# The page table of the paged cache, read as whole rows in an earlier stage

## The chip, the core and the metric

The program runs on one core of a Trainium2 chip. A core has a matrix engine (PE in the profile, with its weight loads shown apart as PEld), three engines for element work (DVE, ACT and POOL), and SP, which here only issues transfers (the row "SPq" of a profile is its issuing of one). The metric is the device time of one execution in microseconds (us). The kernel before took 2102.95, 2104.4 and 2106.95 us in three runs, median 2104.4.

## What is computed

The reference is one inference step of a small trunk of two layers, in float32. Layer 0 is a Mamba-2 mixer, layer 1 is multi-head latent attention (MLA). A prompt of 1024 tokens and 8 sampled sequences of 8 new tokens each go through the same parameters; the sampled sequences have 2048 old tokens each, held in a cache of pages of 128 tokens:

```python
h = h + Mixer_i(RMSNorm(h))            # i = 0: Mamba-2, i = 1: MLA; then a final RMSNorm
cache_ckv  (1, N_POOL, 128, 256)       # paged key/value latents
cache_kpe  (1, N_POOL, 128, 32)        # paged rotary keys
page_table (8, 16) int32               # logical page -> physical page, one row per sequence
```

The page table is what matters for this change. The 128 entries, one for each page of each sequence, say which physical pages belong to the 8 sequences. The kernel turns them into addresses at two places. The rotary keys of all 128 pages are gathered with the 128 entries as they stand, one for each of the 128 partitions. The latents are gathered later in pieces of four pages (512 tokens): sequence b, piece q takes the entries b·16 + 4q + 0 to 3. For this the kernel wants a table of indices with 128 partitions and 32 columns. Column 4b + q belongs to one piece; partition 32j + s holds 32 · page_table[b, 4q + j] + s, so a page is fetched as 32 rows of four tokens. It needs, in partitions 32j to 32j + 31, every fourth entry of the flat page table, starting with the j-th.

## The kernel before

Layer 0 takes the first part of the program, layer 1 the rest. Layer 1 begins with the input stage, `mla_in`. It first normalises the rows of the residual and transposes them in three groups of token tiles (`norm_steps`, `norm_cols`). For each group and each of 8 slices of 128 columns, PE transposes three token tiles into a PSUM tile `xtp` (L234), ACT writes the high part `hh` from it (L235), and DVE writes the low part `hl`, which is the rest that the rounding of `hh` leaves (L236). The products in this stage are three-part sums of high and low parts, which is why each tensor comes as a pair. The `xtp` tiles have three PSUM buffers in turn, so the transposes for slice 3 wait until `hl` of slice 0 has been written, those for slice 4 wait for `hl` of slice 1, and so on. The gate products `pj` (L88) of the same stage are interleaved with the transposes of the next group.

Then `gather_kpe` loads the 128 page-table entries as one column (`kpidx`, L1351) and POOL issues the indirect gather of the rotary keys into `kprows` (L1353). PE transposes those rows a little later (`kpt`, L1362).

After further projections the stage comes to `mla_cq` and `mla_q`. `mla_cq` forms the normalised query latent tile by tile. The last transposed tile passes through a buffer `cqs` (L991) and is split into `cqh` (ACT, L129) and `cql` (DVE, L130). The very last, 64-row tile is folded: ACT copies one half of a PSUM tile into an SBUF tile `pq` (L111), DVE adds the other half (L112). That SBUF tile shares the single buffer of `cqs`, so the copy at L111 waits until `cql` has been computed from it. `mla_q` multiplies the query latent by its weights (PE, `pq`, L100); the result goes through `qt` (ACT, L1012), gets its rotation on DVE (L1018 to L1021), and is stored in DRAM as `q_d` by SP (L1022). `qt` has two buffers, so the third `qt` waits for the first store to land. Between these products the first head group is prepared: the weights `w` are loaded (L1109, L1111) and split (L129, L130), and PE forms the values `vp` (L88). The PSUM tile of `vp` comes from the same three buffers that the folded tile occupies.

The table of indices for the latents is built in `Sample.__init__`, which stands in the program after `mla_q`. It loads the page table with four transfers into 32 partitions each (`ptab`, L1379), each taking every fourth entry, then loads a column of slot numbers (`pslot`, L1381), converts the table to float (`ptf`, L1383), multiplies and adds (L1384) and converts back (`ptidx`, L1386). The first gather that uses it comes in the sampled part of the attention, over 400 us later.

The order of the instructions on DVE, ACT and SP is not written out by hand at this place. A scheduler orders them by its own estimate of when operands are ready, so an instruction may stand earlier in its engine's queue than its text in the program. Each engine then takes its own queue strictly in order, and a waiting instruction holds up all that stand behind it. That is how the loads of `ptab` come to be issued, and `ptf` to be computed, in the middle of `mla_cq` and `mla_q`.

Of the kernel before, what the change touches and what calls it, by code (L numbers as in the profile page):

```python
# [8 lines left out]
F32 = mybir.dt.float32  # L9
F32R = mybir.dt.float32r  # L10
AF = mybir.ActivationFunctionType
ALU = mybir.AluOpType
# [6 lines left out]
NB = 8  # L19
# [17 lines left out]
NPG = PAST // PAGE  # L37
# [649 lines left out]
def h_loader(k):  # L687
    def load(xt, i):
        t0, m = TILES[i]
        k.nc.sync.dma_start(xt[:m], k.h_d[t0 : t0 + m])  # L690

    return load
# [174 lines left out]
def mla_in(k, right, mid):  # L867
    tc, nc, I = k.tc, k.nc, k.I
    k.g_d = k.dram.tile([8, 128, T], F32, name="g_d")
    with ExitStack() as st:  # L870
        xp = st.enter_context(open_pool(tc, name="hT", bufs=1))
        k.xh = xp.tile([128, 8, T + 64], F32R, name="hh")
        k.xl = xp.tile([128, 8, T], F32R, name="hl")

        rw = st.enter_context(open_pool(tc, name="rw", bufs=1))
        sg = ExitStack()
        wg = sg.enter_context(open_pool(tc, name="wpg", bufs=1))
        with k.h0, open_pool(tc, name="h1", bufs=1, side="right") as p0:
            first = [gate_block(k, wg, rw, 0), gate_block(k, wg, rw, 1)]
            norm_steps(k, h_loader(k), k.normc[1], k.xh, k.xl, p0, k.psum, first, 3, tail=True)  # L880
            for b in first:
                next(b, None)
        mp = k.mps.enter_context(open_pool(tc, name="mp", bufs=1, side="right"))
        k.kvh = mp.tile([128, 2, SEQ], F32R, name="kvh")
        k.kvl = mp.tile([128, 2, SEQ], F32R, name="kvl")
        k.kvs = [k.cm.tile([128, 2, 64], F32R, name=f"kvs{x}") for x in "hl"]
        gates = (None for b in range(2, 8) for _ in gate_block(k, wg, rw, b))
        with open_pool(tc, name="kg", bufs=1, side="right") as kg:
            gk = gather_kpe(k, kg)
            next(gk)  # L890
            for n in range(QG + 8):
                next(gates)
                if n >= QG:
                    next(gk)
            drain(gk)
        kp = right.enter_context(open_pool(tc, name="kTp", bufs=1, side="right"))
        k.kT = (kp.tile([98, SEQ], F32R, name="kTh0"), kp.tile([98, SEQ], F32R, name="kTl0"))
        hp = mid.enter_context(open_pool(tc, name="hp", bufs=1, side="right"))
        k.cqh = hp.tile([128, 4, T + 64], F32R, name="cqh")
        k.cql = hp.tile([128, 4, SEQ], F32R, name="cql")  # L900
        sp = mid.enter_context(open_pool(tc, name="sp2", bufs=1, side="right"))
        wk = ExitStack()
        wkp = wk.enter_context(open_pool(tc, name="wpk", bufs=1, side="right"))
        wkv = load_cw(k, wkp, rw, 512, 288, "ck")
        drain(gates)
        sg.close()
        wq = st.enter_context(open_pool(tc, name="wpc", bufs=1))
        wcq = load_cw(k, wq, rw, 0, 512, "cw")
        mla_kv(k, sp, wkv)
        wk.close()  # L910
        wu = mid.enter_context(open_pool(tc, name="wu1", bufs=1, side="right"))
        k.wu = wu
        k.wu0 = load_w(k, wu, I["mla_w_uq"][0].rearrange("q h e -> q (h e)")[:, :384], 4, 384, "wq", 1, None, 1)
        mla_cq(k, sp, wcq)
# [380 lines left out]
def drain(g):  # L1295
    for _ in g:
        pass
# [71 lines left out]
        k.kpe_d.append(d)  # L1369


class Sample:
    def __init__(self, k, pool):
        nc, I = k.nc, k.I
        self.k, self.sp = k, None
        pt = pool.tile([128, 32], mybir.dt.int32, name="ptab")
        for j in range(4):
            src = I["page_table"].rearrange("b (q j) -> j (b q)", j=4)[j : j + 1].to_broadcast([32, 32])
            nc.sync.dma_start(pt[32 * j : 32 * j + 32], src)  # L1379
        ps = pool.tile([128, 1], F32, name="pslot")  # L1380
        nc.sync.dma_start(ps, I["c_slot"])  # L1381
        pf = pool.tile([128, 32], F32, name="ptf")
        nc.vector.tensor_copy(pf, pt)  # L1383
        nc.vector.tensor_scalar(pf, pf, 32.0, ps, op0=ALU.mult, op1=ALU.add)  # L1384
        self.idx = pool.tile([128, 32], mybir.dt.int32, name="ptidx")
        nc.vector.tensor_copy(self.idx, pf)  # L1386
        self.items = [(b, q) for b in range(NB) for q in range(4)]
        self.raw, self.hl, self.cT, self.tk = {}, {}, {}, {}
        self.state, self.held, self.new, self.ps = {}, {}, {}, {}
# [403 lines left out]
def layer_mla(k):  # L1793
    tc, nc = k.tc, k.nc
    k.og_d = k.dram.tile([8, 128, SEQ], F32, name="og_d")
    k.npool = k.I["cache_ckv"].shape[1]
    with ExitStack() as st:
        k.q_d = k.dram.tile([T, MH * 96], F32, name="q_d")
        PB.update(PB2)
        k.cm = st.enter_context(open_pool(tc, name="cm", bufs=1))  # L1800
        right, mid, heads, k.mps = ExitStack(), ExitStack(), ExitStack(), ExitStack()
        p2 = ExitStack()
        k.psum = p2.enter_context(open_pool(tc, name="ps2", bufs=1, space=PS))
        mla_in(k, right, mid)
        qp = st.enter_context(open_pool(tc, name="qp", bufs=1))
        k.qlh = qp.tile([128, 2, NB, 128], F32R, name="qlh")
        k.qll = qp.tile([128, 2, NB, 128], F32R, name="qll")
        k.qpr = qp.tile([96, NB, 128], F32R, name="qpr")
        k.mr = qp.tile([128, 256], F32R, name="mr")
        early = ExitStack()  # L1810
        hd = Heads(k, early)
        q0 = ExitStack()
        hd.start(q0)
        early_units = [hd.prep_kv(0)] * 13 + [hd.prep_q(0)] * 5 + [hd.maxpass(0, 0)] * 6
        early_units += [hd.prep_q(1)] * 5 + [hd.maxpass(0, 1)] * 10
        done = 0
        for n, _ in enumerate(mla_q(k, mid)):
            while done < min((n - Q0 + 1) * len(early_units) // (33 - Q0), len(early_units)):
                next(early_units[done], None)
                done += 1  # L1820
        q0.close()
        mid.close()
        p2.close()
        psum = heads.enter_context(open_pool(tc, name="ps3", bufs=1, space=PS))
        hd.open(heads, psum)
        sm = Sample(k, qp)
        with tc.manual_schedule(engines={nc.tensor.engine, nc.gpsimd.engine}):
            flow = mla_heads(k, hd, sm, early, st)
        heads.close()
        right.close()  # L1830
        with tc.manual_schedule(engines={nc.tensor.engine, nc.gpsimd.engine}):
            mla_sample(k, sm, flow)
        k.mps.close()
# [59 lines left out]
```

## Time and profile before

| | |
|---|---|
| runs (us) | 2102.95, 2104.4, 2106.95; median 2104.4 |
| span of the profiled execution | 2095.4 us; the page gives no other time for that execution, so the runs lie 7.6 to 11.6 above it (median 9.0) |
| mean granted clock of PE | 0.969 of full speed |
| DVE busy | 1340.1 us (64%) |
| ACT busy | 1043.3 us (50%) |
| POOL busy | 851.9 us (41%) |
| data moved | 207.61 MB, 99 GB/s on average |

A timeline row gives start and duration of an instruction or of a run of equal ones, the engine, line and operation, the tiles written and read, the shape, and in brackets how long the engine had been idle before it and what ended that idle time. A row of the chain of waits is one link of the chain of work that ended last: the link's start, its duration and its engine or transfer. A row of the waits by engine names the waiting instruction, then the one that released it, then the total idle time, the number of times and the longest. Durations of matmuls overlap, so their pace is read from the distance of their starts.

### The profile page before, as it was taken

To read this page: it belongs to the slowest core of one execution; us is meant where nothing else is said; L and a number is where in the kernel's file an instruction comes from. 1 tells how busy PE (TensorE), PEld (TensorE's weight loads), DVE (VectorE), ACT (ScalarE), POOL (GpSimd) and SP (SyncE) were. 2 spreads that over 40 slices of the span, in tenths; PEclk is the share of its full clock that TensorE was granted. 3 is DMA by queue.
4 is the path that set the end of the run, shared out by engine and by line. 5 is a ranking of instruction groups with operands and counts; after the bars stand their busy time and mean duration, and the time that the engine had idled before them with its cause. 6 is when DMAs were issued, how large, how long until landed. Compare 5 with 4: busy or idle time off the path is not lost.

```text
span 2095.4 us, 33766 instructions
## 1 busy us (share of the span) xinstructions
PE 1948.3 (93%) x12001; PEld 1763.6 (84%) x12001; DVE 1340.1 (64%) x2838; ACT 1043.3 (50%) x2287; POOL 851.9 (41%) x1059
## 2 busy tenths in 40 slices
PE   6999999999999999789998999699999999889998
PEld 5898999899999998677787998698888888778887
DVE  4558676767676767865334314366787778776665
ACT  5455565556565656522114323234676667755552
POOL 0337564646664646744000001102343334765541
PEclk9999999999999999889999999899999989999999
DMA  4222324231324241635534342132111112464451
GB/s 144 56 59 64 111 66 115 56 114 57 105 66 115 56 115 46 208 122 192 183 124 133 124 152 63 52 108 68 48 55 52 43 37 61 133 197 131 142 152 40
DMA packets 187631, 207.61 MB, mean 99 GB/s; under 512 B 23260, under 2 KB 153064, under 8 KB 187080
## 3 DMA queue, kind: packets, MB, share of 16 engines
q1 hardware_dynamic: 182408, 185.67, 29.2%
q0 software_dynamic: 4976, 19.66, 3.0%
q8 instruction: 95, 1.56, 0.3%
q14 instruction: 72, 0.59, 0.1%
q10 hardware_dynamic: 80, 0.13, 0.0%
HBM read 152.10 MB, written 53.28 MB: 98 GB/s over the span
## 4 chain that ended last, share of the span: by engine, by line
PE 33%; DVE 9%; issue 4%; POOL 4%; DMA 3%; ACT 2%; SPq 0%; POOLq 0%; DVEq 0%; ACTq 0%
PE pq L100 5%; PE pob L100 5%; PE pj L88 4%; PE poa L100 2%; POOL kvl L1541 2%; PE pk L100 1%; PE p L100 1%; PE vp L88 1%; PE st L1246 1%; DVE tl L1260 1%; PE st L1248 1%; PE st L1247 1%; PE o L1277 1%; PE sc L1214 1%; PE kp L88 1%
## 5 line engine op out<-in xcount | busy, mean ns | idle before, releaser
L88 PE MATMUL pj<-xh,wih 128*128 128x384 f32 (+1 forms) x768 | 254.9, 336 | 10.9 <-ACT xh L235 6.6
L88 PE MATMUL pj<-xl,wih 128*128 128x384 f32 (+1 forms) x768 | 255.9, 333 | 0.0
L88 PE MATMUL pj<-xh,wil 128*128 128x384 f32 (+1 forms) x768 | 255.1, 332 | 0.0
L1260 POOL TENSOR_TENSOR tl<-P,th 128x384 fp32r<-128x384 f32 (+1 forms) x96 | 90.7, 945 | 181.0 <-ACT P L1258 138.5
L88 PEld LDWEIGHTS pj<-xh,wih 128*128 128x128 f32 x768 | 145.8, 191 | 12.5 <-ACT xh L235 7.5
L468 DVE SCALAR_TENSOR_TENSOR acc<-raw,vec,acc 128x1112 f32<-128x1112 f32 x96 | 147.0, 1535 | 11.9 <-ACT acc L465 11.1
L88 PEld LDWEIGHTS pj<-xh,wil 128*128 128x128 f32 x768 | 146.3, 190 | 0.6
L88 PEld LDWEIGHTS pj<-xl,wih 128*128 128x128 f32 x768 | 146.1, 190 | 0.5
L575 DVE TENSOR_SCALAR M<-M,tok 128x128 f32<-128x128 f32 (+1 forms) x288 | 116.6, 462 | 43.0 <-DMA M<-acs_d 35.7
L100 PE MATMUL pz<-wih,xh 128*128 128x256 f32 x504 | 143.0, 287 | 0.0
L100 PE MATMUL pz<-wil,xh 128*128 128x256 f32 (+1 forms) x504 | 142.8, 287 | 0.0
L1257 ACT ACTIVATE th<-st 128x512 fp32r<-128x512 f32 x192 | 94.1, 490 | 73.6 <-PE st L1253 54.7
L100 PE MATMUL pz<-wih,xl 128*128 128x256 f32 x448 | 128.1, 286 | 0.0
L130 DVE TENSOR_TENSOR wil<-wraw,wih 128x512 fp32r<-128x512 f32 x88 | 70.4, 802 | 65.7 <-ACT wih L129 63.1
L1541 POOL TENSOR_TENSOR kvl<-pgr,kvh 128x1024 fp32r<-128x1024 f32 x32 | 78.2, 2445 | 67.8 <-ACT kvh L1540 67.8
L100 PEld LDWEIGHTS pz<-wih,xh 128*128 128x128 f32 x504 | 96.0, 190 | 1.1
L577 ACT ACTIVATE M<-M 128x512 f32<-128x512 f32 (+1 forms) x72 | 43.8, 608 | 102.0 <-DVE M L575 101.7
L1258 ACT ACTIVATE P<-st 128x512 f32<-128x512 f32 x192 | 93.2, 486 | 0.0
L100 PEld LDWEIGHTS pz<-wil,xh 128*128 128x128 f32 (+1 forms) x504 | 92.9, 184 | 0.3
L663 POOL TENSOR_TENSOR y<-y,nw 128x256 f32<-128x256 f32 (+1 forms) x72 | 64.5, 896 | 70.2 <-ACT xD L662 69.7
L582 PEld LDWEIGHTS py<-xdt,M 128*128 128x128 f32 (+1 forms) x576 | 70.4, 192 | 19.8 <-DVE xdt L555 6.5
L100 PEld LDWEIGHTS pz<-wih,xl 128*128 128x128 f32 x448 | 85.4, 191 | 0.4
(819 smaller groups left out, 6461.6 us busy)
## 6 DMA issues: line engine op xcount, KB each, us to landing
wraw<-in_ssd_w_in SPq DMA_DIRECT2D x92, 256.0 KB
M<-acs_d SPq DMA_DIRECT2D x64, 256.0 KB
s<-in_state_ssm SPq DMA_DIRECT2D x32, 256.0 KB
y_d<-y SPq DMA_DIRECT2D x64, 128.0 KB
out_s_ssm<-s SPq DMA_DIRECT2D x32, 256.0 KB
wraw<-in_ssd_w_out SPq DMA_DIRECT2D x16, 512.0 KB
q_d<-qt SPq DMA_DIRECT2D x32, 192.0 KB
qp<-q_d SPq DMA_DIRECT2D x8, 768.0 KB
```

What stands on the lines that cost most here:

```text
L88: nc.tensor.matmul(out, a, b, start=(i == 0), stop=(i == n - 1))
L100: nc.tensor.matmul(o, a, b, start=(j == 0), stop=(j == len(ops) - 1))
L130: (eng or nc.vector).tensor_tensor(lo, src, hi.bitcast(F32), op=ALU.subtract)
L468: nc.vector.scalar_tensor_tensor(acc, raw[:, j : j + n], k.convw[j][:, blk : blk + 1], acc, op0=ALU.mult, op1=ALU.add)
L575: nc.vector.tensor_scalar(M[:m, h, :m], M[:m, h, :m], tk[:, 0, 4 * g + h : 4 * g + h + 1], 0.0, op0=ALU.subtract, op1=ALU.min)
L577: nc.scalar.activation(M[:m, :, :m], M[:m, :, :m], AF.Exp)
L582: nc.tensor.matmul(py[:m, h * 64 : h * 64 + 64], M[:m, h, :m], xdt[:m, h * 64 : h * 64 + 64], start=True, stop=True)
L663: nc.gpsimd.tensor_tensor(y[:m], y[:m], nw[:m], op=ALU.mult)
L1257: nc.scalar.activation(th[:, :n], ps[:, :n], AF.Exp, scale=SCALE)
L1258: nc.scalar.activation(P[:, :n], ps[:, :n], AF.Exp, scale=SCALE)
L1260: eng.tensor_tensor(tl[:, :n], P[:, :n], th[:, :n].bitcast(F32), op=ALU.subtract)
L1541: nc.gpsimd.tensor_tensor(rl, raw, rh.bitcast(F32), op=ALU.subtract)
```

## The change

A new function `page_rows` is called in `mla_in` right after the gather of the rotary keys has been started. It loads the whole page table, 128 entries, into every partition with one broadcast transfer (`ptab`, now 128 x 128), and the column of slot numbers. Four DVE copies, one for each group of 32 partitions, pick every fourth entry and convert it to float; the multiplication, the addition and the conversion back follow as before. The resulting `ptidx` stays in a pool that lives through layer 1, and `Sample` takes it from there. The four strided loads, the load of `pslot` and the three DVE operations at the old place are gone.

```diff
         with open_pool(tc, name="kg", bufs=1, side="right") as kg:
             gk = gather_kpe(k, kg)
             next(gk)
+            page_rows(k, kg)
             for n in range(QG + 8):
...
+def page_rows(k, pool):
+    nc, I = k.nc, k.I
+    pt = pool.tile([128, NB * NPG], mybir.dt.int32, name="ptab")
+    nc.sync.dma_start(pt, I["page_table"].rearrange("b p -> (b p)").partition_broadcast(128))
+    ps = pool.tile([128, 1], F32, name="pslot")
+    nc.sync.dma_start(ps, I["c_slot"])
+    pf = pool.tile([128, 32], F32, name="ptf")
+    for j in range(4):
+        r = slice(32 * j, 32 * j + 32)
+        nc.vector.tensor_copy(pf[r], pt[r].rearrange("p (x j) -> p j x", j=4)[:, j])
+    nc.vector.tensor_scalar(pf, pf, 32.0, ps, op0=ALU.mult, op1=ALU.add)
+    k.ptidx = k.cm.tile([128, 32], mybir.dt.int32, name="ptidx")
+    nc.vector.tensor_copy(k.ptidx, pf)
...
 class Sample:
-    def __init__(self, k, pool):
-        nc, I = k.nc, k.I
+    def __init__(self, k):
         self.k, self.sp = k, None
-        pt = pool.tile([128, 32], mybir.dt.int32, name="ptab")
-        for j in range(4):
-            src = I["page_table"].rearrange("b (q j) -> j (b q)", j=4)[j : j + 1].to_broadcast([32, 32])
-            nc.sync.dma_start(pt[32 * j : 32 * j + 32], src)
-        ps = pool.tile([128, 1], F32, name="pslot")
-        nc.sync.dma_start(ps, I["c_slot"])
-        pf = pool.tile([128, 32], F32, name="ptf")
-        nc.vector.tensor_copy(pf, pt)
-        nc.vector.tensor_scalar(pf, pf, 32.0, ps, op0=ALU.mult, op1=ALU.add)
-        self.idx = pool.tile([128, 32], mybir.dt.int32, name="ptidx")
-        nc.vector.tensor_copy(self.idx, pf)
+        self.idx = k.ptidx
...
-        sm = Sample(k, qp)
+        sm = Sample(k)
```

Lines up to 890 keep their numbers in the changed kernel; those from 891 to 1371 move down by one, those from 1391 on by five.

The orders of PE, ACT and POOL stay as they were. Those of SP and DVE change, at two places each. On SP at the old place, between the weight loads of `mla_q` (`wraw`) and of the first head group (`w`) and the stores `q_d`, the kernel before has:

```order
510 L1111 DMA w_14635<-in_mla_w_uv 128x2x256
511 L1379 DMA ptab<-in_page_table 32x32x1 x4
512 L272 DMA wraw<-in_mla_w_uq 128x4x384
513 L1381 DMA pslot<-in_c_slot 128x1
514 L1111 DMA w_14635<-in_mla_w_uv 128x2x256
515 L1022 DMA q_d<-qt_14666 128x384
```

And the changed kernel:

```order
510 L1055 DMA mk<-in_c_maskn 128x256
511 L1110 DMA w_14646<-in_mla_w_uk 128x2x256
512 L1112 DMA w_14647<-in_mla_w_uv 128x2x256
513 L272 DMA wraw<-in_mla_w_uq 128x4x384
514 L1112 DMA w_14647<-in_mla_w_uv 128x2x256
515 L1023 DMA q_d<-qt_14678 128x384
```

The five table transfers are gone from there, and the weight loads and the stores follow each other.

On DVE at the old place the kernel before has the first conversion of the table ahead of the low part of the query latent, and the other two operations further back:

```order
1287 L1019 TENSOR_TENSOR w_14682<-qt_14666,sint 128x128
1288 L130 TENSOR_TENSOR w_14641<-w_14635,w_14640 128x512
1289 L1383 COPY ptf<-ptab 128x32
1290 L130 TENSOR_TENSOR cql<-cqs_14576,cqh 128x4x128
1291 L1020 TENSOR_TENSOR qt_14666<-u_14681,w_14682 128x4x16
1292 L1021 TENSOR_TENSOR qt_14666<-u_14681,w_14682 128x4x16
1293 L1018 TENSOR_TENSOR u_14703<-qt_14688,cost 128x128
1294 L1019 TENSOR_TENSOR w_14704<-qt_14688,sint 128x128
1295 L112 TENSOR_TENSOR pq_14597<-pq_14597,pq_14580 64x512
```

And the changed kernel:

```order
1290 L1020 TENSOR_TENSOR w_14694<-qt_14678,sint 128x128
1291 L130 TENSOR_TENSOR w_14653<-w_14647,w_14652 128x512
1292 L130 TENSOR_TENSOR cql<-cqs_14588,cqh 128x4x128
1293 L1021 TENSOR_TENSOR qt_14678<-u_14693,w_14694 128x4x16
1294 L1022 TENSOR_TENSOR qt_14678<-u_14693,w_14694 128x4x16
1295 L1019 TENSOR_TENSOR u_14715<-qt_14700,cost 128x128
1296 L1020 TENSOR_TENSOR w_14716<-qt_14700,sint 128x128
1297 L112 TENSOR_TENSOR pq_14609<-pq_14609,pq_14592 64x512
```

`cql` follows the second `w` split directly, with nothing about the table ahead of it.

At the new place, SP issues the two transfers behind `kpidx` and ahead of the first store of a gate block (`g_d`), and DVE does the work between the second and the third group of the transposed rows. On SP, as a difference:

```order
 L272 DMA wraw<-in_mla_w_in 128x288 x4
 L272 DMA wraw<-in_mla_w_in 128x512 x2
-L1351 DMA kpidx<-in_page_table 128x1
+L1352 DMA kpidx<-in_page_table 128x1
+L1376 DMA ptab<-in_page_table 128x128
+L1378 DMA pslot<-in_c_slot 128x1
 L854 DMA g_d<-gt_12782 128x1088
```

Two transfers have come in behind `kpidx`, which has only changed its line. And DVE there, again as a difference, where the names `xtp_0` to `xtp_2` with width 320 are the first slices of the third group:

```order
 L236 TENSOR_SCALAR hl<-xtp_7_12884,vec,hh 128x384
+L1382 COPY ptf<-ptab 32x32 x4
+L1383 TENSOR_SCALAR ptf<-ptf,pslot 128x32
 L236 TENSOR_SCALAR hl<-xtp_0_12956,vec,hh 128x320
+L1385 COPY ptidx<-ptf 128x32
 L236 TENSOR_SCALAR hl<-xtp_1_12962,vec,hh 128x320
 L236 TENSOR_SCALAR hl<-xtp_2_12968,vec,hh 128x320
```

Five operations on the table now stand ahead of `hl` of slice 0 of that group, and one between slices 0 and 1.

## The prediction

> **What bounds the kernel now.** I read the busy times on the page first, then the waits by engine, then the chain of waits around the loads of the table, and last the timelines of the engines there. The page says that PE is the engine to look at:
>
> ```profile
> span 2095.4 us, 33766 instructions
> PE 1948.3 (93%) x12001; PEld 1763.6 (84%) x12001; DVE 1340.1 (64%) x2838; ACT 1043.3 (50%) x2287; POOL 851.9 (41%) x1059
> ```
>
> PE is busy 93% of the span, so a stage is worth what it makes PE wait or run slowly. PE's waits, sorted by their total, begin with this one:
>
> ```profile
> PE vp L88 <- DVE pq L112: 16.3, 1, 16.3
> ```
>
> After the line's names come the total, the number of times and the longest: it is a single wait of 16.3 us, and no other line of PE reaches that total with all its waits. The chain of waits follows it back:
>
> ```profile
> 1330.06 20.21 DMA ptab<-in_page_table
> ...
> 1350.57 0.60 DVE cql L130
> ...
> 1352.64 1.62 PE vp L88 x6
> ```
>
> The last of the four `ptab` transfers has 20.21 us in the chain, from 1330.06. Behind it DVE converts the table, makes `cql`, rotates, and folds `pq`; only then may PE go on with `vp`. The timelines of PE, DVE, ACT and SP over the same stretch:
>
> ```profile
> 1335.83 0.40 PE L88 MATMUL vp<-w,kvh 128*128 128x256 f32 x2
> 1336.07 0.28 PE L88 MATMUL vp<-w,kvl 128*128 128x256 f32 x1
> 1352.64 0.77 PE L88 MATMUL vp<-w,kvh 128*128 128x256 f32 x2 [16.29 <-DVE pq L112]
> ...
> 1355.85 0.34 PE L100 MATMUL pq<-wqh,cql 128*128 128x384 f32 x1
> 1356.03 0.34 PE L100 MATMUL pq<-wqh,cqh 128*128 128x384 f32 x1
> ```
>
> ```profile
> 1331.95 0.68 DVE L130 TENSOR_TENSOR w<-w,w 128x512 fp32r<-128x512 f32 x1
> 1350.39 0.18 DVE L1383 CAST ptf<-ptab 128x32 f32<-128x32 int32 x1 [17.75 <-DMA ptab<-in_page_table]
> 1350.48 0.68 DVE L130 TENSOR_TENSOR cql<-cqs,cqh 128x512 fp32r<-128x512 f32 x1
> ...
> 1352.69 0.23 DVE L1384 TENSOR_SCALAR ptf<-ptf,pslot 128x32 f32<-128x32 f32 x1
> 1353.58 0.48 ACT L1012 COPY qt<-pq 128x384 f32<-128x384 f32 x1 [0.33 <-DMA q_d<-qt]
> 1326.09 10.45 SPq L1379 DMA_DIRECT2D ptab<-in_page_table  x4
> 1336.64 2.94 SPq L272 DMA_DIRECT2D wraw<-in_mla_w_uq  x1
> 1339.62 6.16 SPq L1381 DMA_DIRECT2D pslot<-in_c_slot  x1
> 1345.89 1.56 SPq L1111 DMA_DIRECT2D w<-in_mla_w_uv  x1
> 1351.46 1.69 SPq L1022 DMA_DIRECT2D q_d<-qt  x2
> ```
>
> DVE had nothing to wait for but the table: its last work began at 1331.95, and `cql` started the moment the conversion let it, 0.09 us later. The four table transfers also occupy SP's issuing for 10.45 us. While they run, almost nothing arrives, as the transfers from 1326 to 1352 show (the rate in 40 slices of 0.65 us each, and the sizes):
>
> ```profile
> GB/s 255 14 1 1 1 1 1 1 1 1 1 1 1 1 1 1 1 1 1 1 1 1 1 1 26 1 1 0 0 1 27 78 126 171 216 241 317 247 125 46
> ...
> wraw<-in_mla_w_uq SPq DMA_DIRECT2D x1, 768.0 KB
> w<-in_mla_w_uv SPq DMA_DIRECT2D x1, 256.0 KB
> ```
>
> The window of the work that follows the stall (columns: length, then busy time and count of PE, PEld, DVE, ACT and POOL, then PE's granted clock):
>
> ```profile
> 1352.60:1355.90 3.30, 3.26 (x12) 3.15 (x13) 2.41 (x13) 2.90 (x8) 0.54 (x1) 0.52 0.24 89
> ```
>
> For 3.3 us the clock is at 0.52, and 12 matmuls are all that fall there. The slow transfer is 4 x 32 x 32 = 4096 entries picked one by one. From the first issue (1326.09) to the end of the last (1350.27) that is 24.2 us, 5.9 ns an entry.
>
> **The change, part by part.** *Old place, the stall.* PE could go on at 1336.07 + 0.12 = 1336.19 (the two `vp` at 1335.83 and the one at 1336.07 start 0.12 apart) and goes on at 1352.64: 16.45 us go.
>
> *Old place, the clock.* From 1352.64 to 1355.85 PE starts the 12 of the window less the one at 1355.85: six `vp` (the chain has their count) and five `pq`. At the full pace (0.12 apart for `vp`, 0.18 for `pq` from 1355.85 to 1356.03) they would take 6 x 0.12 + 5 x 0.18 = 1.6 us, and took 3.2. So 1.6 us go as well, 18.05 in all. The three DVE operations that leave (0.6 us) lie in that stretch and are worth nothing apart.
>
> *What is late next there.* DVE starts `cql` at 1331.95 + 0.60 = 1332.55, and from the start of `cql` to `vp` it took 1352.64 - 1350.48 = 2.16 us, so `vp` could start at 1334.7, 1.5 us ahead of PE's need. That cover is ample. The next `pq` needs its PSUM tile emptied by the third `qt` copy, and this waits for the first `q_d` store to land. In the rows, the store is issued at 1351.46 and the copy starts at 1353.58, 2.12 later. It was issued 0.98 us after `cql` began, which now makes 1333.5. So the copy can start at 1335.6 and ends by 1336.1, while PE needs it after the six `vp`, at 1336.9. But SP now issues 768 KB (`wraw`) and 256 KB (`w`) just ahead of that store; the buffer of `w` is read by DVE until about 1332.6 (1331.95 + 0.6). At the 317 GB/s of the fastest slice above, 1 MB takes 3.3 us: from about 1331 to 1334.3, or to 1336 if the buffers come late. The store then lands as late as 1337 to 1338. I take 0.3 us of waiting, with 0 and 2 as its ends: the copy's own cover is 0.8 us, and the loads are mostly ahead of the store.
>
> *New place.* These rows (SP, POOL, DVE, PE) show where the five new operations and the two transfers fall:
>
> ```profile
> 1154.32 0.42 SPq L1351 DMA_DIRECT2D kpidx<-in_page_table  x1
> 1171.83 0.33 SPq L854 DMA_DIRECT2D g_d<-gt  x1
> 1158.11 1.17 POOL L1353 DMA_INDIRECT kprows<-in_cache_kpe,kpidx  x1 [8.75 <-PE xtp L234]
> 1157.29 0.55 DVE L236 SCALAR_TENSOR_TENSOR hl<-xtp,vec,hh 128x320 fp32r<-128x320 f32 x1 [1.86 <-ACT hh L235]
> 1160.27 1.70 DVE L236 SCALAR_TENSOR_TENSOR hl<-xtp,vec,hh 128x320 fp32r<-128x320 f32 x3 [1.11 <-ACT hh L235]
> 1159.09 1.73 PE L234 MATMUL xtp<-ident,xt 128*128 128x128 f32 x9
> ```
>
> SP is idle from 1154.74 to 1171.83, so the two issues delay no other transfer, and `kpidx` stays ahead of them. POOL's gather needs `kpidx` alone: it has landed by 1158.11, at most 3.8 us after its issue. That is the price I take for each new transfer: `ptab` issued at 1154.8 lands by 1158.6, and `pslot`, issued about 0.4 us behind it, by 1159.0. The 128 rows of the broadcast would add 128 x 5.9 ns = 0.75 us at the old pace, and I put this into the upper end. DVE then waits in front of `hl` of slice 0 instead of doing it at 1157.29. After the landing come four copies at 0.09 each (the distance of the two starts at 1350.39 and 1350.48) and the multiplication at 0.23: `hl` of slice 0 starts at 1159.2 and ends at 1159.75; with `ptidx` (0.1) and another 0.55, slice 1 ends at 1160.4. Who waits: the nine transposes at 1159.09 are slices 2, 3 and 4, about 0.58 us each; slice 3 (due at 1159.65) needs `hl` of slice 0, slice 4 (due at 1160.2) that of slice 1. So PE loses 0.1 to 0.2 us. Later slices are late by as much, since DVE has them in a row from 1160.27 anyway. I take 0.3 us, with 0 (the transfers land a microsecond sooner) and 3 (they land 1.5 us later, and the clock goes down too, below) as the ends. The bytes grow from 16 KB to 64 KB, nothing beside the 2 MB of the gather behind.
>
> The Trainium skill, "DMA: Bandwidth & Descriptors", section "Latency and other measured facts", speaks of a fixed cost of about 2 us for a DMA. By that estimate both transfers would land by 1157.3, `hl` of slice 0 would be done by 1158.5, PE would lose nothing here, and the time would be 2086.6. The trace has 2.12 us for the store above and at most 3.8 for `kpidx`, the nearer relative of the two new ones, so that I keep the longer figure.
>
> *Sum.* 16.45 + 1.6 - 0.3 - 0.3 = 17.45 us, 2095.4 - 17.45 = 2077.95 as a span. The profiled execution's span lies 9.0 below the median of the runs; with that put on, the time is 2104.4 - 17.45 = 2086.9 us, 0.83% faster. The work after 1360 is a sequence of the same instructions and moves forward as a whole; the first use of `ptidx` is far behind both places.
>
> **The rivals.** *A. The stall moves in part.* A wait at the new place ends in a halved clock, or the store at the old place lands late. The trace shows that a stall much shorter than the old one is enough:
>
> ```profile
> 1146.47 0.44 PE L88 MATMUL pj<-hh,wgh 128*128 128x384 f32 x1 [1.91 <-ACT gt L849]
> ...
> 1148.57 0.52 PE L88 MATMUL pj<-hl,wgh 128*128 128x384 f32 x1
> 1148.89 0.52 PE L88 MATMUL pj<-hh,wgl 128*128 128x384 f32 x1
> ```
>
> After 1.91 us of idleness the products start 0.32 apart instead of 0.17. So if the transfers land 2 us later than I take, PE loses about 2 us and some 1.6 on the clock, and with 1 to 2 at the store the gain is 13 to 16 us: 2089 to 2092. The Trainium skill, "TensorE: Matmul & The Clock Gate", Part 1, puts the limit for a halved clock at an idle window of about 3.4 us; by that, a stall of 2 us would cost nothing more and the case would end at 2089 or 2090. The row at 1148.57 speaks against it.
>
> *B. Slower: the broadcast lands as slowly as the old table.* DVE then sits on `ptab` or `pslot` with all of `hl` behind it, PE stops at slice 3, and the gain is spent 190 us earlier. From the landing to the release of slice 3 it takes 0.36 + 0.23 + 0.55 = 1.1 us. If the transfer takes the whole 24.2 us from 1154.8, it lands at 1179.0, PE stands from 1159.65 to 1180.1, 20.5 us, and loses 1.6 on the clock: 22.1 against 18.05, or 2108.8 with the store. It decides for "slower" from a landing at about 1175, 20 us after issue. For it speaks that `pslot` held SP for 6.16 us in its old place; against it, that this was in a queue full of single entries, that `kpidx`, also 128 single entries, took at most 3.8 us, and that a row of 512 bytes is one piece and not 128.
>
> *C. No change.* The stage could be held by something else that ends as late, the `w` load (issued at 1345.89) or the first `q_d` store. Then the time stays at about 2104. Against it: those are late because SP was held by the table, and the chain names no other link.
>
> **Chances.** The forecast 0.74, A 0.16, B 0.06, C 0.04. My own case runs from 2083.5 (nothing lost, 18.05 gained, the shortest run 1.5 below the median, and up to 1.5 for where changes of clock fall) to 2089. The range takes in A's time and the ends of the two unknown costs: 2083 to 2092. About 0.2% (4 us) is what a measurement of this kernel can tell from no change: faster 0.90, same 0.04, slower 0.06.
>
> **What would show it.** In the changed profile: no wait of PE above 3 us between 1300 and 1360; `cql` 0.1 us behind the second `w` split; `vp` without a gap; PE's clock at 1.00 there; and at the new place an idle time of DVE of about 3 us ended by `ptab` or `pslot`, with less than 0.5 us of PE idleness ahead of the third or fourth slice's transposes. The prediction is wrong if that DVE wait ends after 1161, if the copies cost more than 0.2 us each, or if PE waits for the `q_d` store after `vp`.

## The result, and the profile after

The changed kernel took 2081.84 us (median of 4 runs, 2076.78 to 2088.45), the kernel before, measured beside it, 2103.68 us (2101.3 to 2106.95). The ratio is 0.9905 with a 95% interval of 0.988 to 0.993; it is not the quotient of the two medians, which is 0.9896 here. In a second measurement, beside some of the experiments below, it was 0.9949 (0.9928 to 0.997), 2086.49 against 2096.36 us. Executions of one kernel lie up to 25 us apart, and the two measurements differ by more than most steps of the change are worth. So the work below is read from the traces, by place, and the times serve as a check on the sum. One execution of the kernel before, of 29 measured beside the first four experiments below, took 3298.5 us at a mean clock of 0.702 and is left out of the ratios.

The page of the changed kernel begins with its span; the waits of PE no longer contain `vp` and begin with another line; and the last row is the first and last start of all transposes `cqp` of `mla_cq`, from the view by source line:

```profile
span 2079.4 us, 33770 instructions
PE 1947.1 (94%) x12001; PEld 1760.8 (85%) x12001; DVE 1341.5 (65%) x2841; ACT 1041.2 (50%) x2287; POOL 852.6 (41%) x1059
...
PE nmp L1230 <- DVE nm L1227: 14.7, 11, 2.0
...
L989 PE MATMUL cqp<-ident,cq x36: 222/272/328, 1290.4 to 1340.5; 128*128 128x128 f32 x32, 64*128 64x64 f32 x4
```

The same row of the kernel before:

```profile
L988 PE MATMUL cqp<-ident,cq x36: 222/272/328, 1291.7 to 1357.4; 128*128 128x128 f32 x32, 64*128 64x64 f32 x4
```

PE's order is the same in both, and these 36 transposes enclose the old place. The stretch took 65.7 us before and 50.1 us after: 15.6 us went there. The timelines of PE, DVE, ACT and SP at that place show how:

```profile
1335.48 0.28 PE L88 MATMUL vp<-w,kvl 128*128 128x256 f32 x1
1337.92 0.45 PE L100 MATMUL pq<-wqh,cqh 128*128 128x384 f32 x1 [2.16 <-ACT qt L1013]
1338.21 0.34 PE L100 MATMUL pq<-wql,cqh 128*128 128x384 f32 x1
...
1330.63 0.68 DVE L130 TENSOR_TENSOR w<-w,w 128x512 fp32r<-128x512 f32 x1
1331.23 0.68 DVE L130 TENSOR_TENSOR cql<-cqs,cqh 128x512 fp32r<-128x512 f32 x1
...
1337.39 0.48 ACT L1013 COPY qt<-pq 128x384 f32<-128x384 f32 x1 [3.39 <-DMA q_d<-qt]
...
1329.13 0.37 SPq L272 DMA_DIRECT2D wraw<-in_mla_w_uq  x1
1331.34 0.37 SPq L1112 DMA_DIRECT2D w<-in_mla_w_uv  x1
1332.22 10.73 SPq L1023 DMA_DIRECT2D q_d<-qt  x5
```

`cql` follows the split of `w` by 0.6 us, its own start distance, and `vp` goes through without a gap. Then PE waits 2.16 us for the third `qt` copy, which waits for the first `q_d` store: issued at 1332.22, it released the copy at 1337.39, 5.2 us later. The transfer rate from 1328 to 1341 (40 slices of 0.325 us) shows what lay in its way:

```profile
GB/s 0 0 0 0 0 0 9 85 80 128 326 388 406 411 392 342 249 366 339 292 312 213 33 9 19 22 24 28 14 0 0 0 0 0 0 19 350 236 0 0
```

The weight loads and the first stores move at 250 to 410 GB/s from 1331.3 to 1334.8. A tail at 10 to 30 GB/s follows from 1335.2 to 1337.4, and the copy starts when it ends. The tail is the work of a single one of the core's 16 DMA engines, as two windows of the transfers show, the first from 1334.25 to 1335.18, the others from 1335.30 to 1337.35 (after the queue's name its packets, its MB and the share of the 16 engines' time):

```profile
q8 instruction: 1, 0.02, 6.3%
...
DMA packets 33, 0.04 MB, mean 19 GB/s; under 512 B 3, under 2 KB 33, under 8 KB 33
q1 hardware_dynamic: 33, 0.04, 6.5%
```

One engine of 16 is 6.25%. By their sizes in the trace, the 33 packets are one engine's part of three transfers, one behind the other: 16 of `w`, 8 of the first store, 8 of the second, and a small one at the end of each. The other engines wrote fifteen such small ones for the first store by 1334.66, 2.4 us after its issue; the sixteenth came at 1336.84. The late packets begin when a 16 KB packet of the queue for instructions ends (1334.25 to 1335.18), and the second trace of the changed kernel has the same order. That this packet held up the late engine is likely, but not shown: the trace does not say which engine carried a packet.

The new place, SP, DVE and PE:

```profile
1153.19 0.36 SPq L1376 DMA_DIRECT2D ptab<-in_page_table  x1
1153.59 0.43 SPq L1378 DMA_DIRECT2D pslot<-in_c_slot  x1
...
1156.91 0.77 DVE L1382 CAST ptf<-ptab 32x32 f32<-32x32 int32 x4 [3.10 <-DMA ptab<-in_page_table]
1157.71 0.24 DVE L1383 TENSOR_SCALAR ptf<-ptf,pslot 128x32 f32<-128x32 f32 x1
1157.86 0.54 DVE L236 SCALAR_TENSOR_TENSOR hl<-xtp,vec,hh 128x320 fp32r<-128x320 f32 x1
...
1158.46 1.22 PE L234 MATMUL xtp<-ident,xt 128*128 128x128 f32 x6 [0.43 <-DVE hl L236]
```

DVE waits 3.10 us for the table, PE 0.43 us for `hl` of slice 0. By the two places the change is worth 15.6 - 0.4 = 15.2 us, 0.72% of 2104, between the two measured ratios.

### The profile page after: what moved, and what is told of

It is laid out like the page before. It is cut to its first block, busy times and chain, and to the rows that moved or that the text cites. A ratio compares the mean times of both kernels' runs of the same rounds, so it can differ in the third digit from the quotient of the medians.

```text
span 2079.4 us, 33770 instructions
## 1 busy us (share of the span) xinstructions
PE 1947.1 (94%) x12001; PEld 1760.8 (85%) x12001; DVE 1341.5 (65%) x2841; ACT 1041.2 (50%) x2287; POOL 852.6 (41%) x1059
## 5 line engine op out<-in xcount | busy, mean ns | idle before, releaser
L582 PE MATMUL py<-xdt,M 128*128 128x64 f32 (+1 forms) x576 | 75.6, 276 | 10.8 <-DVE xdt L555 6.9
```

Source lines behind the costliest of these rows:

```text
L582: nc.tensor.matmul(py[:m, h * 64 : h * 64 + 64], M[:m, h, :m], xdt[:m, h * 64 : h * 64 + 64], start=True, stop=True)
```

## The experiments

My theory: what cost the time was the reading of single entries, both through DVE's wait for it and through the queue that it filled; the place matters only as far as something waits for the table there. The rivals: the earlier place alone does it; DVE's wait alone was the cost; the cost of an early table comes back elsewhere. The table gives the measured times, beside before on the same chip, and two numbers of each trace: the stretch from the first to the last `cqp`, and the longest idle time of PE at the place that the run was about.

| run | median us | before | ratio (95%) | `cqp` stretch us | PE's wait us |
|---|---|---|---|---|---|
| changed kernel, first | 2081.84 | 2103.68 | 0.9905 (0.988 to 0.993) | 50.1 | 2.16 |
| changed kernel, again | 2086.49 | 2096.36 | 0.9949 (0.9928 to 0.997) | 51.5 | 2.12 |
| form alone | 2090.64 | 2098.76 | 0.9951 (0.9927 to 0.9975) | 54.5 | 3.78 |
| place alone | 2100.31 | 2098.76 | 0.9995 (0.9971 to 1.0019) | 51.7 | 13.00 at `kpt` |
| late conversion | 2098.38 | 2098.76 | 1.0004 (0.9982 to 1.0027) | 66.1 | 16.21 |
| early rows | 2088.32 | 2098.76 | 0.9945 (0.9914 to 0.9976) | 51.9 | 2.18 |
| third `qt` | 2081.99 | 2096.36 | 0.9933 (0.9909 to 0.9956) | 50.9 | 2.27 |
| store through POOL | 2084.52 | 2096.36 | 0.9943 (0.9921 to 0.9966) | 48.9 | 1.02 |
| early rows, third `qt` | 2086.07 | 2096.36 | 0.9942 (0.9923 to 0.9962) | 50.2 | 0.91 |
| third and fourth `qt` | 2081.83 | 2097.97 | 0.9923 (0.9896 to 0.9951) | 48.3 | none |
| early rows, third and fourth `qt` | 2080.94 | 2097.97 | 0.9919 (0.9893 to 0.9946) | 49.0 | none |
| half the entries | 2096.4 | 2097.97 | 0.9986 (0.9962 to 1.0009) | 65.2 | 14.12 |
| entries spread | 2097.93 | 2102.8 | 0.9985 (0.996 to 1.001) | 49.5 | 13.54 at `kpt` |

**The form alone.** The broadcast, issued from the last tile of `mla_cq`; since memory there is short, `ptab` takes a buffer of the squares.

```diff
-            page_rows(k, kg)
...
         if m == 64:
+            page_rows(k, sp)
             pq, pq_ = sp.tile([128, 512], F32, tag="cqs", name="pq8", bufs=1), pq
```

> One broadcast of whole rows as in the changed kernel, but issued where the old loads were (in the last tile of mla_cq), with the DVE work at its old place too. If the form of the transfer is what counts, the table lands within 5 us of its issue, DVE finds it there before cql, PE's wait at vp is gone, and the time is that of the changed kernel within 2 us (0.990 to 0.994 of before). If the earlier place is what counts, DVE still waits ahead of cql by several us and most of the 16 us come back (0.997 or more).

SP, DVE, POOL and PE of this run:

```profile
1321.17 0.35 SPq L1377 DMA_DIRECT2D ptab<-in_page_table  x1
1324.28 2.24 DVE L1383 CAST ptf<-ptab 32x32 f32<-32x32 int32 x4 [2.07 <-DMA ptab<-in_page_table]
1326.56 0.98 DVE L1384 TENSOR_SCALAR ptf<-ptf,pslot 128x32 f32<-128x32 f32 x1
...
1324.56 1.00 POOL L1070 MEMSET Vh<- 128x1024 f32 x1 [2.53 <-PE pq L100]
1326.54 1.88 POOL L1061 MEMSET qTl<- 2x1024 f32 x2
...
1335.29 0.69 PE L100 MATMUL pq<-wqh,cqh 128*128 128x384 f32 x1 [3.78 <-ACT qt L1014]
1335.78 0.52 PE L100 MATMUL pq<-wql,cqh 128*128 128x384 f32 x1
```

The table landed 3.1 us after its issue, where the single entries took 24. The stretch fell to 54.5 us, so 11.2 of the 15.6 us belong to the form alone. The other 4.4 belong to the place: DVE waited 2.07 us, the four copies and the multiplication took 3.2 us while POOL was writing zeros, and with the scheduler's order these stood ahead of the `cql` of the tile before, so all of DVE came later. PE waited 3.78 us and went on at half pace. The measured ratio of 0.9951 lies above the expected 0.990 to 0.994, and DVE did not find the table there: of the expectation, the short landing and the end of PE's wait at `vp` came true.

**The place alone.** In `page_rows` the old four loads and the one conversion stand in place of the broadcast and the four copies:

```diff
-    nc.sync.dma_start(pt, I["page_table"].rearrange("b p -> (b p)").partition_broadcast(128))
+    for j in range(4):
+        src = I["page_table"].rearrange("b (q j) -> j (b q)", j=4)[j : j + 1].to_broadcast([32, 32])
+        nc.sync.dma_start(pt[32 * j : 32 * j + 32], src)
```

> The old four loads of single entries, at the new place. The scheduler puts the DVE work ahead of hl of slice 7 there. If the form counts, the table lands 24 to 27 us after the first issue at about 1153, so DVE reaches that hl at about 1179 to 1180 and PE, which needs it at about 1166.5, stands for 13 to 14 us and loses 1 to 2 on the clock: the gain of the changed kernel shrinks from 15 us in the trace to 0 to 3. If the place counts, nobody waits there for more than 2 us and the time is that of the changed kernel.

SP, DVE and PE, and the landing time of the gather:

```profile
1155.80 13.60 SPq L1378 DMA_DIRECT2D ptab<-in_page_table  x4
...
1182.78 0.18 DVE L1382 CAST ptf<-ptab 128x32 f32<-128x32 int32 x1 [15.64 <-DMA ptab<-in_page_table]
1182.42 1.08 PE L1363 MATMUL kpt<-ident,kprows 128*128 128x128 f32 x4 [13.00 <-DMA kprows<-in_cache_kpe,kpidx]
DMA to landing us min/median/max: 22.2/22.2/22.2
```

The table was used 27.0 us after the first issue, and PE stood for 13.00 us: the gain is gone, and the time is that of before. The size came out as expected, the releaser did not. The single entries also held up the gather of the rotary keys, 22.2 us to landing against 8.3 before, and PE came to `kpt` while DVE still waited. This is the stall of rival B of the prediction, brought about by the old form of the loads: an early place is worth nothing if the table lands late.

**The conversion late, the loads where they were.** The kernel before, with DVE's three operations moved to `begin`, where the last heads start:

```diff
-        nc.vector.tensor_copy(pf, pt)
-        nc.vector.tensor_scalar(pf, pf, 32.0, ps, op0=ALU.mult, op1=ALU.add)
...
+        pf = sp.tile([128, 32], F32, name="ptf")
+        nc.vector.tensor_copy(pf, self.ptab)
+        nc.vector.tensor_scalar(pf, pf, 32.0, self.pslot, op0=ALU.mult, op1=ALU.add)
```

> The kernel before, with the four loads of single entries where they were, but the DVE work on the table moved some 400 us back, so that no DVE instruction waits for it near cql. If DVE's wait is all that cost time, 14 to 18 us are gained. If the loads also hold up the queue behind them, the first q_d store is issued only after 1347 and lands at about 1353; the third qt copy waits for it, PE stands from about 1336.9 to 1353.5, and the gain is 0 to 3 us.

DVE, SP, ACT and PE:

```profile
1328.15 0.68 DVE L130 TENSOR_TENSOR cql<-cqs,cqh 128x512 fp32r<-128x512 f32 x1
1335.27 6.30 SPq L1381 DMA_DIRECT2D pslot<-in_c_slot  x1
1341.67 0.89 SPq L1111 DMA_DIRECT2D w<-in_mla_w_uv  x1
1342.60 9.24 SPq L1022 DMA_DIRECT2D q_d<-qt  x4
1348.35 0.48 ACT L1012 COPY qt<-pq 128x384 f32<-128x384 f32 x1 [17.42 <-DMA q_d<-qt]
1348.88 0.69 PE L100 MATMUL pq<-wqh,cqh 128*128 128x384 f32 x1 [16.21 <-ACT qt L1012]
```

DVE's wait is gone and nothing is gained. `cql` is made at 1328.15, but SP is held in its issues by the single entries and issues the store at 1342.60, more than 13 us after `qt` was ready (1329.1), and PE waits 16.21 us for the copy behind it, as long as it had waited for DVE. The chain of waits of the kernel before had named one wait; behind it stood another of the same cause that ends as late. The rival "DVE's wait alone" falls.

**The rows early.** `page_rows(k, xp)` ahead of the input stage's loop in place of the call after the gather.

> The changed kernel with the table read and converted before the MLA input stage, at the end of layer 0, so that hl of the third group waits for nothing. The wait of PE of 0.43 us at the transposes near 1158 goes; elsewhere nothing changes unless DVE at the end of layer 0 holds up its residual additions. 0.4 us less than the changed kernel, which the timing cannot tell from it: 0.988 to 0.994 of before. If that wait had cost more than it shows (a clock or a later wait), 1 to 3 us less.

The wait near 1158 is not in this trace. The time is that of the changed kernel within its interval, as expected. The wait at the store is the same, 2.18 us; this time PE ran slowly after it, and the stretch took 51.9 us, 1.8 more than the first trace of the changed kernel.

**The changed kernel again.**

> The changed kernel once more, beside the three below. From the trace its own two places are worth 15.2 us (15.6 at the old, less 0.4 at the new): 0.991 to 0.995 of before. The wait of about 2.2 us for the first q_d store is there again; whether the clock goes down after it is open (it did not in the first profile and did with the early table), and with it the gain at the old place is 15.6 or about 13.7 us.

PE after the same wait, and a window of it (columns as in the prediction, PE's clock third from the end):

```profile
1337.48 0.69 PE L100 MATMUL pq<-wqh,cqh 128*128 128x384 f32 x1 [2.12 <-ACT qt L1013]
1337.40:1341.40 4.00, 3.92 (x14) 3.67 (x15) 2.58 (x11) 1.81 (x6) 0.00 (x0) 0.58 0.24 88
```

The same stall, 2.16 and 2.12 us, once left the clock at 1.00 and once brought it to 0.58 for the next 4 us. The price was 1.4 us (51.5 against 50.1), and 1.8 us in the run with the early rows. At the new place no wait of PE shows in this trace, against 0.43 us in the first; in the three later runs whose order there is the same it was 0.18, 0.20 and 0.52 us.

**A third buffer for `qt`.** The third tile goes to a buffer of `mla_cq` that is free by then:

```diff
             qt = sp.tile([128, 4, 96], F32, tag="qt", name=f"qt{c}{i}", bufs=2)
+            if (c, i) == (0, 2):
+                qt = k.sp2.tile([128, 512], F32, tag="cq", name="qt02", bufs=2)[:, :384].rearrange("p (h e) -> p h e", h=4)
```

> The changed kernel with a buffer of its own for the third qt tile of mla_q, so that its copy does not wait for the first q_d store to land. If that store is what PE waits for, its wait of 2.2 us at pq goes below 0.5, nothing of that size takes its place before 1360, and 2 to 4 us are gained on the changed kernel (0.989 to 0.993 of before). If another operand is late at the same time (vp or the next store), the wait comes back within the next two pq tiles and less than 1 us is gained. The scheduler orders some later transposes and products differently, which may cost or gain up to 1 us.

PE's wait was still 2.27 us. The third tile's copy was free, but the scheduler had put the fourth tile's copy ahead of it in ACT's order, and that one waits for the same store. This run does not test the cause; it shows only that a buffer has to be counted through the new order.

**The store through POOL.** The first two stores are issued by POOL, on its own queue:

```diff
-            nc.sync.dma_start(k.q_d[t0 : t0 + m, cs], qf[:m])
+            (nc.gpsimd if (c, i) in ((0, 0), (0, 1)) else nc.sync).dma_start(k.q_d[t0 : t0 + m, cs], qf[:m])
```

> The changed kernel with the first two q_d stores issued by POOL through its own queue, not behind the 1 MB of weight loads on SP's. If the place in SP's queue makes the store late, it now lands 2.5 to 3.5 us after qt is ready and PE's wait at pq is 0 to 0.7 us. If the data paths themselves are busy with the loads, the store lands as late as before, about 5 us after its issue, and the wait stays at 2 us or more.

POOL, ACT and PE:

```profile
1332.13 0.65 POOL L1023 DMA_DIRECT2D q_d<-qt  x1 [1.12 <-DVE w L1020]
1335.64 0.48 ACT L1013 COPY qt<-pq 128x384 f32<-128x384 f32 x1 [2.25 <-DMA q_d<-qt]
1336.17 0.44 PE L100 MATMUL pq<-wqh,cqh 128*128 128x384 f32 x1 [1.02 <-ACT qt L1013]
```

The store was through 3.5 us after its issue, not 5.2, and the wait fell from 2.16 to 1.02 us: a little outside the band of 0 to 0.7. Whether the queue of its own did this is not shown. Fifteen engines had ended the store by 1334.11, 2.0 us after its issue, and the sixteenth, again behind its packets of `w`, at 1335.08. On that engine the store ended 0.5 us after `w` in both runs; the 1.7 us lie in the end of its `w`, 4.1 us after the store's issue in the changed kernel and 2.5 us here. The 16 KB packet ended earlier here too, 1.3 us after the store's issue and not 3.0.

**Third and fourth buffer.** The fourth tile takes the buffer of the squares, which is free too; then the same with the early rows.

```diff
+            if c == 0 and i in (2, 3):
+                tag, bufs = ("cq", 2) if i == 2 else ("sqq", 1)
+                qt = k.sp2.tile([128, 512], F32, tag=tag, name=f"qt0{i}", bufs=bufs)[:, :384].rearrange("p (h e) -> p h e", h=4)
```

> The changed kernel with buffers of their own for the third and the fourth qt tile, since ACT's order had the fourth ahead of the third, and the fourth still waited for the first q_d store. Now no copy waits for that store until the fifth tile. If the store is what PE waits for at pq, its wait of 2.1 to 2.3 us there goes below 0.5 us, PE has no idle time of over 1 us from 1320 to 1360, and the stretch from the first to the last cqp transpose takes 47.5 to 48.5 us (50.1 and 51.5 in two traces of the changed kernel). If something else is late, a wait of over 1 us stays or comes within two tiles.

> The table read at the end of layer 0 and a third qt buffer: neither of the two waits that the changed kernel has left is there. By the trace 0.4 + 2.2 us, and up to 1.9 of the clock, less than the changed kernel: 17.5 to 20 us below before, 0.989 to 0.993. If the early reading costs anything at the end of layer 0 it is seen as idle time of PE there.

> The table read at the end of layer 0 and own buffers for the third and fourth qt tile. By the traces 0.4 us at the transposes and 2.1 to 4 us at the stores less than the changed kernel: 17.5 to 20 us below before, 0.989 to 0.993. Executions of one kernel lie up to 10 us apart, so that the timing can tell this from before but hardly from the changed kernel; the trace tells it, with no wait of PE over 1 us between 1320 and 1360 and none near 1158.

The row by source line of the run with both buffers:

```profile
L990 PE MATMUL cqp<-ident,cq x36: 222/272/328, 1288.6 to 1336.9; 128*128 128x128 f32 x32, 64*128 64x64 f32 x4
```

With both buffers no idle time of PE is left from 1318 to 1375, and the stretch takes 48.3 us: the store was what PE waited for, and it cost 1.8 to 3.2 us. The run with the early rows and the third buffer alone had kept a wait of 0.91 us for the reason above. The last version has neither of the two waits; its ratio of 0.9919 is the lowest of the runs made beside it, but its interval overlaps that of the changed kernel, so that only the traces say it is better. At 49.0 us its stretch is longer than that with both buffers alone, without a wait of PE in it.

**What makes the single entries slow.** Two runs, which settle less than I had hoped. First, half as many entries in the same four loads of the kernel before:

```diff
-            src = I["page_table"].rearrange("b (q j) -> j (b q)", j=4)[j : j + 1].to_broadcast([32, 32])
-            nc.sync.dma_start(pt[32 * j : 32 * j + 32], src)
+            src = I["page_table"][:4].rearrange("b (q j) -> j (b q)", j=4)[j : j + 1].to_broadcast([32, 16])
+            nc.sync.dma_start(pt[32 * j : 32 * j + 32, :16], src)
```

> The kernel before, with the same four strided loads at the old place, each of half as many single entries (the table's first four sequences; the columns of the other four are copies, so the sampled attention of those reads the wrong pages). If each entry costs about 5.9 ns, the table lands about 12 us after its first issue, PE's wait at vp falls from 16.3 to 4 to 5 us, with 1 to 4 us of waiting for the store behind it, and the stretch from the first to the last cqp transpose from 65.7 to 53 to 57 us. If the cost lies in the four transfers and not in the entries, the wait stays at 14 us or more.

SP, DVE and PE:

```profile
1326.08 1.95 SPq L1379 DMA_DIRECT2D ptab<-in_page_table  x4
1348.20 0.17 DVE L1383 CAST ptf<-ptab 128x16 f32<-128x16 int32 x1 [15.57 <-DMA ptab<-in_page_table]
1350.45 0.77 PE L88 MATMUL vp<-w,kvh 128*128 128x256 f32 x2 [14.12 <-DVE pq L112]
```

SP's issues of the table shrank from 10.45 to 1.95 us, though the load of `pslot` behind them then held SP for 9.36. The table was used 22.1 us after the first issue, against 24.3 with all entries. So a price for each entry, which the prediction had worked out as 5.9 ns, does not exist in that form. The transfers do not stand still meanwhile: from 1330 to 1340 the kernel before moved 2168 packets of under 512 bytes and this run 1095, so half the entries came at half the pace. Why the pace halved is not shown. Second, in the run with the place alone, the entries written 64 bytes apart:

```diff
-    pt = pool.tile([128, 32], mybir.dt.int32, name="ptab")
+    pt = pool.tile([128, 32, 16], mybir.dt.int32, name="ptab")[:, :, 0]
```

> The four loads of single entries at the new place as in the run with the place alone, but each entry is written 64 bytes from the next one in its partition, not 4. In that run DVE's first operation on the table began 27.0 us after the first load's issue, and the gather took 22.2 us to land. Halving the entries had not halved the time, so what counts may be where they are written: if writes of 4 bytes into the same short piece of a partition wait for each other, the table now lands within 14 us of the first issue, the gather within 14 us, and PE's wait at kpt falls from 13.0 to under 5 us. If the time lies in the reading of the same few bytes of the page table, or in the single transfer as such, both numbers stay within 3 us of what they were.

SP, DVE and PE:

```profile
1155.14 13.26 SPq L1378 DMA_DIRECT2D ptab<-in_page_table  x4
1182.68 0.19 DVE L1382 CAST ptf<-ptab 128x32 f32<-128x32 int32 x1 [16.20 <-DMA ptab<-in_page_table]
1182.32 1.08 PE L1363 MATMUL kpt<-ident,kprows 128*128 128x128 f32 x4 [13.54 <-DMA kprows<-in_cache_kpe,kpidx]
```

27.5 us against 27.0: writing the entries 64 bytes apart did not help. What sets the pace stays open, the reading of the same few bytes or something in the single transfer; over the four loads it makes 5.5 to 6.9 us each in these four traces. That whole rows avoid it is shown: 3.1 and 3.7 us from issue to use.

## Why the prediction was right, and where it was off

*The stall and the clock at the old place (16.45 + 1.6 us).* Right, by the same rows: the stretch lost 15.6 us, and with the 2.16 us of the new wait added back 17.8 stand against the 18.05 that were worked out. The kernel with the store's wait gone too took 48.3 us, 17.4 less than before.

*What is late next there (0.3 us, ends 0 and 2).* Right in kind, wrong in size: this is the term that was mis-sized. It measured 2.16 and 2.12 us, just above the upper end, and the clock added up to 1.4. That PE waits for the `q_d` store after `vp` was also one of the prediction's own signs of being wrong. The copy's cover of 0.8 us held only if the store landed 2.1 us after its issue as before. It took 5.2. I had put the loads' end between 1334.3 and 1336 from a peak rate, and then taken the near end. For fifteen of the 16 engines that was right: they ended the store 2.4 us after its issue, which by estimate (the copy started 0.5 us after the store's last packet, PE 0.5 us after the copy) would have cost PE nothing. The sixteenth was 2.2 us later, and a transfer has landed only when its last engine is through. The prediction had no term for this. In the kernel before, the 16 KB packet ran from 1341.80 to 1342.73, inside the stall (the slice of 26 GB/s in the prediction's row), where almost nothing else moved.

*The new place (0.3 us, ends 0 and 3).* 0 to 0.52 us in five traces. `ptab` was there 3.7 us after its issue (3.8 taken) and `pslot` by the time DVE came to it. The copies took 0.19 us each, twice the 0.09 of the estimate, which was read off the distance of two unlike operations.

*The sum.* 17.45 us predicted, 15.2 by the traces of the two places, 21.8 and 9.9 by the two pairs of medians. Put on the median of 2104.4 us from which the range of 2083 to 2092 was made, the first ratio gives 2084.4, the second 2093.7 and the traces' sum 2089.2. The forecast of 2086.9 stands in the middle of these, but the second ratio lies above the range and the traces' sum where rival A's time begins, so that it is partly luck how close the first measurement came. That a measurement of this kernel can tell 4 us was too hopeful: the 95% interval of the first ratio is about 10 us wide. The prediction put the profiled execution's span 9.0 us below the runs. In every run here that has both numbers the time is 1.7 to 2.1 us above the span, so that execution itself took about 2097 us: about 7 of the 9.0 were spread between runs, not a part of the time. Since the gain was taken from the median, the forecast did not hang on it.

*The rivals.* A is what happened in part, at the store and not at the new place, and the traces' sum of 15.2 us lies in the 13 to 16 that it was given. B did not happen; its stall was brought about with the single entries at the new place. It cost 13.0 us of standing, not the 20.5 worked out, since the scheduler put DVE's work further back there, and it came through the gather. C, "held by something else that ends as late", was given 0.04 with the argument that the `q_d` store was late only because the table held SP. That argument is shown: with DVE's wait taken away alone nothing was gained, and the change gained because it took the queue's load away with it.

## What to carry to other kernels

A wait in the chain can have a second wait behind it that ends at almost the same time: before its removal is counted as a gain, follow every queue that the same cause fills, here SP's issues and the store behind them. A small table that is gathered entry by entry can cost more than one that is read whole and picked apart on chip, 24 us against 3 to 4 here, and moving the slow form to an earlier place only moves the stall. When a stage is made earlier, look at the next transfer it waits for with the loads that now run ahead of it, and take the time until the last engine has moved its part of them, not the rate at their peak.

## What was not expected of the hardware

*The clock after a short stall is not a function of the stall.* 2.16 us of idleness left it at 1.00, 2.12 us brought 0.58 for the next 4 us, in the same kernel at the same place; with the third buffer 2.27 us left it at 1.00. The Trainium skill, "TensorE: Matmul & The Clock Gate", Part 1, says that activity is judged in a window of about 3.4 us that runs freely, so that it depends on where in the window a change falls; the traces agree with that, and not with a fixed limit on the stall, as the prediction had weighed it. In them the clock changes in steps of 3.41 us, at 1145.90 and 1149.31 in the first trace and at 1337.33 and 1340.74 in the second. Counted on from there, the first trace's stall falls into two steps and the second's almost wholly into one (columns as in the prediction):

```profile
1333.63:1337.04 3.41, 2.14 (x18) 1.93 (x16) 0.15 (x1) 0.37 (x2) 0.54 (x1) 1.00 0.41 146
```

```profile
1333.92:1337.33 3.41, 1.44 (x13) 1.23 (x11) 0.00 (x0) 0.38 (x2) 0.54 (x1) 1.00 0.21 73
1337.33:1340.74 3.41, 3.26 (x10) 3.26 (x11) 2.58 (x11) 1.89 (x6) 0.00 (x0) 0.50 0.16 58
```

PE was busy 2.14 us of the emptiest step in the first and 1.44 in the second. With the third buffer it was 1.60, and the clock stayed; with the early rows it was 1.23, and the next step ran at 0.50. These are figures of this place alone.

*Most of the spread between three traces lies where nothing was changed.* First and last start of the transposes `nmp` of the attention, for the first trace of the changed kernel, the form alone, and the early rows with both buffers:

```profile
L1230 PE MATMUL nmp<-ident,nm x32: 269/273/376, 1380.1 to 1771.6; 128*8 128x128 f32 x32
```

```profile
L1231 PE MATMUL nmp<-ident,nm x32: 269/273/377, 1384.9 to 1787.7; 128*8 128x128 f32 x32
```

```profile
L1234 PE MATMUL nmp<-ident,nm x32: 269/273/376, 1380.9 to 1765.6; 128*8 128x128 f32 x32
```

391.5, 402.8 and 384.7 us, at a mean clock over the whole program of 0.973, 0.965 and 0.979. The spans of these traces lie 22.2 us apart, 18.1 of them here; that is more than the change itself, and a median of few runs carries it.

*DVE's small operations took three times as long beside POOL.* A copy of 32 x 32 took 0.19 us in the changed kernel and 0.56 us in the run with the form alone, where POOL was writing zeros at the same time; the multiplication took 0.98 instead of 0.24 (up to 0.47 in other traces of the changed order). The Trainium skill, "SBUF — State Buffer", "SBUF: two separate sides", says that POOL and those DVE operations that use DVE's second port share a pair of ports under an exclusive lock, so that one of them stands while the other's instruction runs. The rows fit that, but no run here shows that these operations are of that kind, or took POOL's work away.
